# A recurrent layer beside a dense matmul stream: state-free products moved out of the chunk loop, and the loop run in step with the next head pair's products

## The chip, the cores and the metric

The kernel runs on one core of a Trainium2 chip. The metric is device microseconds of one execution, the median of three runs. The core has five engines with a queue each, and each queue runs its instructions in the order in which they were built: TensorE (PE) multiplies matrices into PSUM, VectorE (DVE) and ScalarE (ACT) do elementwise work and read PSUM, GpSimd (POOL) does a little elementwise work, and SyncE (SP) issues the DMAs.

## The reference

One decoder layer over 512 tokens of width 2048, all in float32. What is computed:

- `z = rmsnorm(x) @ w_in`. Half of the columns feed an RG-LRU branch (a short convolution, two gates, a linear scan over time). The others, mixed with the token before, feed an RWKV-7 branch of 16 heads of width 64.
- For each head the RWKV-7 branch keeps a 64x64 state: `state = state * w_t + (state @ -kk_t) b_t^T + v_t k_t^T`, and `y_t = state @ r_t`. A norm of y by head, a bonus term and a gate follow.
- `h = x + concat(out_a, out_b) @ w_o`, a gated feed-forward block of width 6144 with a short convolution, a gated embedding block, and a last norm.

## The kernel before, in words

**Dense stream.** Every large product is made of 128x128x512 matmuls. A float32 weight tile of 128x1024 arrives by DMA and is split into two float32r parts: ACT writes the high part (`whi`, line 118) and DVE the rest (`wlo`, line 119). Each weight block is then multiplied three times (`dense`, lines 148, 150, 152). Phase 1 (`phase1`, about the first 900 us) makes z, the two branches and the part of the output product that is ready by then; phase 2 is the rest of the layer and is almost wholly dense.

**Eight head pairs.** The 16 heads are handled as 8 pairs j, 128 partitions each. `rwkv_z` makes k, r and v of a pair in the dense stream. `prep(j)` makes decays, the normed key and the tiles `AR`, `bt`, `ktl`. `core(j)` runs the recurrence in 8 chunks of 64 tokens, in three stages:

- scores: four batches of matmuls (line 676), masked by DVE into `MQ` and `NQ` (line 678);
- the inverse `TT` of a triangular 64x64 matrix for each chunk: DVE makes 2x2 blocks (lines 699 to 701), then four doublings of two products each on 32x32 tiles (line 708), each followed on DVE by a mask (`Gm`, line 718) or by an addition and a transpose (`Tm`, `Tt`, lines 732, 733), and two last products (lines 739, 749). Beside it DVE makes token-major copies of v, b and k (`turn`: one 128x512 transpose, then four of 32x256, lines 684, 689);
- the chunk loop. The state passes from chunk to chunk through three pieces of PE work, with an engine between each: `px` from the state (lines 761, 764), copied by ACT to `xs`; `pu = TT @ xs` (line 776), copied by ACT to `us`; then the state's update (lines 782, 788), scaled and added by DVE into `st` (line 796). The output `y` takes three more products (lines 769, 772, 785).

At the end of a core come a norm by head (lines 803 to 812, with two short PE pieces at lines 825 and 844) and a store.

**The order on PE** is set while the program is built. `merge` walks a model of time: it takes dense matmuls one by one, counts 216 ns for each, and puts in the next piece of `prep` or `core` when the latency that the piece before declared (table `W`) is over. So PE's queue is a fixed sequence, in which some five to seven dense matmuls stand between two pieces. On the other engines the framework's scheduler sets the order, with the priorities that `merge` gives.

```python
            if core is not None and cr <= t:
                    with self.tc.high_priority(offset=self.OFFS):
                        pe, lat = next(core)
                    t += pe
                    cr = t + max(lat, self.PACE)
```

**The RG-LRU branch** (`lru_x`, `lru_y`) adds DVE work in bursts: reciprocals in four pieces (`recip`, line 569), a scan (line 908), a convolution (line 861). `per` in `W` says how many of its 16 steps stand between the pairs.

Of the kernel before, what the change touches and what calls it, by code (L numbers as in the profile page):

```python
# [16 lines left out]
W = dict(offw=0, offp=-100, offl=0, pace=1000, offs=200, offd=100, start=2088, lora=2383, dec=0, rsk=12200, ready=11377, bonus=26772, t0=3419, tg=1322, tt=1448, lx=1000, lu=914, ls=1363, g1=1489, g2=3586, g3=4312, per=[4, 2, 2, 3, 1, 4, 0])  # L17
# [62 lines left out]
class Builder:  # L80
# [22 lines left out]
    def wfill_(self):  # L103
        nc = self.nc
        while self.wn < len(self.wq) and len(self.wt) < self.LOOK:
            src, shape, *own = self.wq[self.wn]
            self.wn += 1
            if self.wraw:
                raw = self.wraw.pop(0)
            else:  # L110
                raw = self.t(self.wp, "wraw", shape, bufs=self.RAW)
                nc.sync.dma_start(raw, src)
# [85 lines left out]
    def build(self):  # L198
# [4 lines left out]
        with ExitStack() as top:  # L203
            cp = top.enter_context(tc.tile_pool(name="cp", bufs=1))
# [26 lines left out]
    def phase1(self):  # L231
# [18 lines left out]
        wst = [("gt", 2), ("gt", 2), ("bv", 2), ("bv", 2), ("AR", 2), ("AR", 2), ("MQ", 1), ("NQ", 1)]  # L250
        self.xr, self.wraw = [], []

        def wload():
            i = len(self.wraw)
            src, shape = self.wq[i]
            if i < len(wst):
                w = self.t(k1, wst[i][0], shape, bufs=wst[i][1])
            else:
                w = self.t(self.wp, "wraw", shape, bufs=self.RAW)
# [25 lines left out]

        self.zs = cp.tile([128, S + 1], F32, name="zs")
        G.memset(self.zs[:, 0:1], 0.0)
        self.zc = cp.tile([128, S + 3], F32, name="zc")
# [3 lines left out]
        self.prepped = {}  # L292
        with self.tc.manual_schedule(engines={mybir.EngineType.PE}):
            self.merge(self.dense_stream(self.order))

    def start(self):
        A = self.A

        order = [("lora",), ("r", 0)]
# [4 lines left out]
        for j in range(1, NP):  # L304
            order.append(("r", j))
            for _ in range(per[j - 1]):
                order.append(lseq.pop(0))
# [31 lines left out]
    def merge(self, dn):  # L339
# [5 lines left out]
        ptime = 0.0  # L345
        self.ptime = None
        pr = cr = 0.0
        while True:
            if prep is None and pj < NP and pj in self.zdone and pj <= cj + 1:
                prep, pr = self.prep(pj), t + W['start']  # L350
                pj += 1
            if core is None and cj < NP and cj in self.prepped:
                core, cr = self.core(cj, self.prepped[cj]), max(t, ptime)
            if core is not None and cr <= t:
                try:
# [3 lines left out]
                    cr = t + max(lat, self.PACE)  # L359
# [4 lines left out]
            if prep is not None and pr <= t:  # L364
                try:
                    with self.tc.high_priority(offset=W['offp']):
                        pe, lat = next(prep)
                    t += pe
                    if self.ptime is not None:
                        ptime, self.ptime = t + self.ptime, None  # L370
                    pr = t + lat
# [3 lines left out]
            if more:  # L375
                try:
                    with self.tc.high_priority(offset=self.OFFD):
                        next(dn)
# [4 lines left out]
            if core is None and prep is None and cj >= NP:  # L383
                break
            t = min(x for x, g in ((cr, core), (pr, prep)) if g is not None)

    def dense_stream(self, order):
        nc, A = self.nc, self.A
        done = max(i for i, o in enumerate(order) if o[0] == "y")
        for i, o in enumerate(order):  # L390
# [12 lines left out]
            else:  # L403
                if o[1] == 0:
                    self.out_b(range(4, NP - 1))
# [12 lines left out]
    def derive(self):  # L418
# [4 lines left out]
        der = k1.tile([128, 128], F32, name="der")  # L423
# [57 lines left out]
    def lora_z(self):  # L481
# [25 lines left out]
        for tt in range(4):  # L507
            z = self.t(k1, ("vk", "bk", "kk2", "Tm")[tt], (128, LW), bufs=1)
# [44 lines left out]
    def rwkv_z(self, j):  # L553
        k1 = self.k1
        d = {}
        for n, m_, o_ in (("kt", "mu_k", "mk"), ("rt", "mu_r", "mr"), ("vt", "mu_v", "mv")):
            ps = self.mm()
# [14 lines left out]
    def prep(self, j):  # L572
# [35 lines left out]
        psg = wk()  # L608
        for i, (wt, x0) in enumerate(((lh[:, 2, :], self.g0h), (lh[:, 2, :], self.g0l), (ll[:, 2, :], self.g0h))):
            TE.matmul(psg, wt, x0, start=i == 0, stop=False)  # L610
        TE.matmul(psg, lh[0:96, 3, :], self.g1, start=False, stop=True)
        gt = T("gt", 2)
        SC.activation(gt, psg, AF.Copy)
# [9 lines left out]
        pc = T("pc", 2, (128, NC))  # L623
# [4 lines left out]
        yield 2000, W['rsk']  # L628
# [648 lines left out]
```

## Time and profile before

| | |
|---|---|
| median of three runs | 2790.03 us (2787.96 to 2790.09) |
| the profiled execution's own time | 2788.58 us |
| its span | 2786.5 us |
| PE busy over the span | 2739.8 us (98%) |
| DVE busy | 1349.5 us (48%) |
| ACT busy | 895.6 us (32%) |

The profile shows one execution. A row of a timeline gives the start and the length of an instruction, or of several like it (x4). A PE row's length covers the passage through the array, so that neighbouring matmuls overlap: what a matmul costs the queue is the distance from its start to the next one's. The trace shows each small float32 matmul of the program as two instructions. "PE idle" is time in which no matmul was in the array.

### The profile page before, as it was taken

The numbers are of one execution on the slowest core, as the hardware profiler recorded it, in microseconds if no ns is written. First come the engines' busy times: TensorE is split into PE (matmuls) and PEld (weight loads), VectorE is DVE, ScalarE is ACT, GpSimd is POOL, SyncE is SP. The second block draws the span as 40 slices with busy tenths as digits, with TensorE's granted clock in tenths as the row PEclk, the third lists the DMA queues.
The fourth block names the chain that finished last, engine by engine and source line by source line (L and its number), as shares of the span: only waits on it lengthen the run. The fifth ranks groups of instructions, "written<-read, shape, count | busy, mean of one in ns | idle before, by whom it ended". The sixth has DMA issues, their size and how long they took to land.

```text
span 2786.5 us, 42621 instructions
## 1 busy us (share of the span) xinstructions
PE 2739.8 (98%) x18392; PEld 2195.7 (79%) x18392; DVE 1349.5 (48%) x1793; ACT 895.6 (32%) x1352; POOL 291.4 (10%) x232
## 2 busy tenths in 40 slices
PE   8999999999999999999999999999999999999996
PEld 7777777777777888888888888888888888877886
DVE  7786686677673533333333433334333333344235
ACT  6343343434422422212221222222222212234334
POOL 4010010101121310000000000000000000012013
PEclk9999999999999999999999999999999999999998
DMA  5222222222332322222222222222222223223222
GB/s 169 80 69 77 73 73 66 66 69 69 100 119 92 110 97 93 98 99 98 98 92 99 93 96 98 99 98 94 95 96 94 98 98 99 97 90 112 98 89 101
DMA packets 81885, 261.31 MB, mean 94 GB/s; under 512 B 9504, under 2 KB 12192, under 8 KB 81696
## 3 DMA queue, kind: packets, MB, share of 16 engines
q1 hardware_dynamic: 81696, 258.58, 28.1%
q8 instruction: 144, 2.36, 0.4%
q14 instruction: 45, 0.37, 0.0%
HBM read 250.42 MB, written 8.13 MB: 93 GB/s over the span
## 4 chain that ended last, share of the span: by engine, by line
PE 92%; DVE 4%; issue 1%; POOL 1%; ACT 1%; DMA 1%; SPq 0%; DVEq 0%; POOLq 0%; ACTq 0%
PE mm L150 26%; PE mm L152 26%; PE mm L148 26%; PE mm L1120 2%; PE mm L1122 2%; PE mm L1121 2%; PE wk L708 1%; DVE wlo L119 1%; PE wk L676 1%; PE ch L776 1%; PE ch L761 1%; PE y L785 1%; DVE e L1153 0%; PE wk L825 0%; POOL lt L478 0%
## 5 line engine op out<-in xcount | busy, mean ns | idle before, releaser
L118 ACT ACTIVATE whi<-wraw 128x1024 fp32r<-128x1024 f32 (+2 forms) x449 | 468.6, 1044 | 1443.0 <-PE mm L150 1280.4
L119 DVE TENSOR_TENSOR wlo<-wraw,whi 128x1024 fp32r<-128x1024 f32 (+2 forms) x449 | 555.5, 1237 | 495.7 <-ACT whi L118 490.5
L148 PE MATMUL mm<-uh,whi 128*128 128x512 f32 x1536 | 597.7, 389 | 0.0
L152 PE MATMUL mm<-uh,wlo 128*128 128x512 f32 x1536 | 597.6, 389 | 0.0
L150 PE MATMUL mm<-ul,whi 128*128 128x512 f32 x1536 | 597.5, 389 | 0.0
L150 PE MATMUL mm<-xl,whi 128*128 128x512 f32 x1216 | 486.3, 400 | 0.0
L148 PE MATMUL mm<-xh,whi 128*128 128x512 f32 x1216 | 485.3, 399 | 0.9 <-DVE hT L408 0.9
L152 PE MATMUL mm<-xh,wlo 128*128 128x512 f32 x1216 | 486.0, 400 | 0.0
L152 PEld LDWEIGHTS mm<-uh,wlo 128*128 128x128 f32 x1536 | 288.4, 188 | 60.0
L150 PEld LDWEIGHTS mm<-ul,whi 128*128 128x128 f32 x1536 | 288.4, 188 | 59.8
L148 PEld LDWEIGHTS mm<-uh,whi 128*128 128x128 f32 x1536 | 288.4, 188 | 59.7
L148 PEld LDWEIGHTS mm<-xh,whi 128*128 128x128 f32 x1216 | 228.6, 188 | 49.7 <-issue 2.2
L150 PEld LDWEIGHTS mm<-xl,whi 128*128 128x128 f32 x1216 | 228.5, 188 | 49.1 <-issue 2.1
L152 PEld LDWEIGHTS mm<-xh,wlo 128*128 128x128 f32 x1216 | 228.5, 188 | 48.6 <-issue 2.3
L1068 DVE TENSOR_TENSOR hT<-hT,mm 128x512 f32<-128x512 f32 x96 | 66.0, 688 | 321.4 <-PE mm L152 321.4
L1048 POOL TENSOR_TENSOR tmp<-tmp,rsa 128x512 f32<-128x512 f32 x48 | 62.0, 1292 | 1406.6 <-ACT tmp L1047 1406.6
L150 PE MATMUL mm<-hl,whi 128*128 128x512 f32 x384 | 153.4, 400 | 0.0
L152 PE MATMUL mm<-hh,wlo 128*128 128x512 f32 x384 | 152.2, 396 | 0.0
L148 PE MATMUL mm<-hh,whi 128*128 128x512 f32 x384 | 152.1, 396 | 0.0
L1052 DVE TENSOR_TENSOR tmp<-tmp,mm 128x512 f32<-128x512 f32 x48 | 33.0, 688 | 160.2 <-PE mm L152 158.1
L1042 DVE TENSOR_TENSOR gz<-mm,rsa 128x512 f32<-128x512 f32 x48 | 33.2, 692 | 153.9 <-PE mm L152 153.9
L1120 PE MATMUL mm<-whi,uh 128*128 128x512 f32 (+1 forms) x304 | 107.0, 352 | 0.0
(430 smaller groups left out, 2914.0 us busy)
## 6 DMA issues: line engine op xcount, KB each, us to landing
wraw<-wgu SPq DMA_DIRECT2D x192, 512.0 KB, 3.2
wraw<-wd SPq DMA_DIRECT2D x96, 512.0 KB, 3.2
wraw<-wz SPq DMA_DIRECT2D x80, 512.0 KB, 3.6
wraw<-wpg SPq DMA_DIRECT2D x31, 512.0 KB, 3.2
wraw<-wo SPq DMA_DIRECT2D x24, 512.0 KB, 3.3
wraw<-wo SPq DMA_DIRECT2D x16, 256.0 KB, 2.9
tmp<-xT SPq DMA_DIRECT2D x16, 256.0 KB, 2.7
out<-e SPq DMA_DIRECT2D x16, 256.0 KB, 2.5
```

The costliest lines, as they stand in the source:

```text
L118: nc.scalar.activation(hi, raw, AF.Copy)
L119: nc.vector.tensor_tensor(lo, raw, hi.bitcast(F32), ALU.subtract)
L148: nc.tensor.matmul(ps, hi[:, k, :], xh, start=first and i == 0, stop=False)
L150: nc.tensor.matmul(ps, hi[:, k, :], xl, start=False, stop=False)
L152: nc.tensor.matmul(ps, lo[:, k, :], xh, start=False, stop=last and i == n - 1)
L1042: V.tensor_tensor(gz[:, 2:S + 2], pg, rs, ALU.mult)
L1048: G.tensor_tensor(c, c, rs, ALU.mult)
L1052: V.tensor_tensor(c, c, pu, ALU.mult)
L1068: V.tensor_tensor(hT[m], hT[m], pd, ALU.add)
L1120: TE.matmul(pg[tt], u3[k + i][0][:, ts_], wh[:, i, :], start=k + i == 0, stop=False)
L1121: TE.matmul(pg[tt], u3[k + i][0][:, ts_], wl[:, i, :], start=False, stop=False)
L1122: TE.matmul(pg[tt], u3[k + i][1][:, ts_], wh[:, i, :], start=False, stop=k + i == KT - 1)
```

## The change

- `core` is split in two generators. `batch(j)` holds all that needs no state: scores, inverse, token-major copies, and three batches of 64x64 products that are new (`each`): `X1 = NQ^T v`, `WT` (from the token-major copy `ak` of the key row of `AR`, and `TT`), and `TT` applied to `X1`. `chain(j)` is the chunk loop, which now has two pieces in a chunk: `pu = WT^T st`, to which DVE adds the `X1` of the chunk and so gives `us`; then the state's update. ACT's copies `xs` and `us` are gone.
- `duo(j)` runs `chain(j - 1)` and `batch(j)` in step: one piece of each is put into PE's queue together. The last `chain` runs alone.
- `turn` is as before, and is called four times in place of three (`ak` is new).
- `AR` of the next pair is written only when the running `duo` is through; the dense stream holds its place until a pair is prepared (`need`). The norm becomes a generator of its own (`norm`). The numbers of `W` are others, and the RG-LRU steps are spread 2, 3, 2, 2, 2, 2, 3.
- Buffers: `MQ`, `NQ`, `vk`, `bk`, `kk2` twice; some tiles move to another pool.

```diff
-W = dict(offw=0, offp=-100, offl=0, pace=1000, offs=200, offd=100, start=2088, lora=2383, dec=0, rsk=12200, ready=11377, bonus=26772, t0=3419, tg=1322, tt=1448, lx=1000, lu=914, ls=1363, g1=1489, g2=3586, g3=4312, per=[4, 2, 2, 3, 1, 4, 0])
+W = dict(offw=10000, offp=[0, 0, 2000, 2000, 74, 0, 0], offl=0, offt=0, pace=433, dpace=1779, late=4035, offs=20000, offd=0, start=2863, lora=2837, dec=0, rsk=25495, ready=14000, bonus=26772, t0=3322, tg=2489, tt=1500, lx=3454, lu=739, ls=643, g1=684, g2=3586, g3=5015, per=[2, 3, 2, 2, 2, 2, 3, 0])
...
-                    cr = t + max(lat, self.PACE)
+                    cr = t + max(lat, W['dpace'] if 0 < cj < NP else self.PACE)
...
+    def duo(self, j):
+        two = []
+        if j:
+            two.append(self.chain(j - 1, self.prepped[j - 1], self.batched.pop(j - 1)))
+        if j < NP:
+            two.append(self.batch(j, self.prepped[j]))
+        while two:
+            pe, lat = 0, 0
+            for g in list(two):
+                try:
+                    p_, l_ = next(g)
+                    pe, lat = pe + p_, max(lat, l_)
...
+        def each(lhs, rhs, dst):
+            ps = wk()
+            for c in range(NC):
+                for hs in H2:
+                    TE.matmul(ps[hs, c * C:(c + 1) * C], lhs(hs, c), rhs(hs, c), start=True, stop=True)
+            SC.activation(dst, c3(ps), AF.Copy)
...
+        for half in range(2):
+            scores(bt, MQ, half)
...
+                    ak = turn("ak", fl(AR[:, 0]), 1)
...
+        X1 = NQ[:, :, 0:64]
+        each(lambda hs, c: NQ[hs, c, 0:64], lambda hs, c: vk[hs, c, :], X1)
...
+        WT = MQ[:, :, 0:64]
+        each(lambda hs, c: ak[hs, c, :], lambda hs, c: TT[hs, c, :], WT)
+        each(lambda hs, c: TT[hs, c, :], lambda hs, c: NQ[hs, c, 0:64], X1)
...
             if c:
-                for hs in H2:
-                    TE.matmul(px[hs, 0:64], AR[hs, c, 0, :], st[hs], start=False, stop=True)
-            xs = T("xs", 2, (128, 64))
-            SC.activation(xs, px[:, 0:64], AF.Copy)
...
+                pu = ch()
+                for hs in H2:
+                    TE.matmul(pu[hs, 0:64], MQ[hs, c, 0:64], st[hs], start=True, stop=True)
+                us = T("us", 2, (128, 64))
+                V.tensor_tensor(us, pu[:, 0:64], NQ[:, c, 0:64], ALU.add)
...
-            pu = ch()
-            for hs in H2:
-                TE.matmul(pu[hs, 0:64], TT[hs, c, :], xs[hs], start=True, stop=True)
-            us = T("us", 2, (128, 64))
-            SC.activation(us, pu[:, 0:64], AF.Copy)
```

In the new kernel the scores are at line 723 (mask 725), `each` at 732, the 2x2 blocks at 755 to 757, the doublings at 764 (mask 774, addition 792, transpose 793), the last products at 801 and 814, and `turn` at 738 and 743; in the chain `pu` is at 843, `us` at 845, the state's update at 849 and 858, the output's products at 851, 854 and 869, and `st` at 862 and 866. The norm's PE pieces are at 901 and 920.

**PE's queue, one chunk of the loop.** Before (head pair 1; `ch`, `wk` and `y` are PSUM tiles, lines 148 to 152 are dense matmuls):

```order
L761 MATMUL ch_2908<-vk_2360,NQ_2222 64x64 x2
L764 MATMUL ch_2908<-st_2891,AR_1673 64x64 x2
L769 MATMUL y_2769<-NQ_2222,vk_2360 64x64 x2
L772 MATMUL y_2769<-AR_1673,st_2891 64x64 x2
L148 MATMUL mm_2759<-xh_76_380,whi_2648 128x512
...
L776 MATMUL ch_2924<-xs_2913,TT 64x64 x2
L782 MATMUL ch_2929<-vk_2360,kk_396_2555 64x64 x2
L152 MATMUL mm_2759<-xh_81_403,wlo_2649 128x512
...
L785 MATMUL y_2769<-MQ_2221,us_2927 64x64 x2
L788 MATMUL ch_2929<-us_2927,bk_2453 64x64 x2
```

And in the changed kernel (chunk of pair 1 with the products of pair 2):

```order
L843 MATMUL ch_3602<-st_3552,MQ_2070 64x64 x2
L849 MATMUL ch_3607<-vk_2190,kk_370_2576 64x64 x2
L851 MATMUL y_3270<-NQ_2071,vk_2190 64x64 x2
L854 MATMUL y_3270<-AR_1954,st_3552 64x64 x2
L764 MATMUL wk_3614<-Tm_3304,MQ_3282 32x16 x32
L148 MATMUL mm_3401<-xh_85_423,whi_3260 128x512
...
L858 MATMUL ch_3607<-us_3605,bk_2453 64x64 x2
L869 MATMUL y_3270<-MQ_2070,us_3605 64x64 x2
L764 MATMUL wk_3675<-Gm_3647,Tt_3305 32x16 x32
```

Three runs of small matmuls in a chunk, five dense ones between them, have become two, 9 to 12 apart, and each of the two ends with a batch of 32x32 products that stood alone before.

**DVE's queue, from the masks of the scores to `Tm`.** Before (head pair 2):

```order
L678 TENSOR_TENSOR MQ_3303<-wk_3326,con_157 128x512
L812 TENSOR_TENSOR y_510_3227<-y_510_3227,gt_1413 128x512
L699 TENSOR_TENSOR Tt_3372<-MQ_3303,con_157 32x256 x4
L678 TENSOR_TENSOR NQ_3304<-wk_3341,con_157 128x512
L700 TENSOR_TENSOR Tt_3372<-Tt_3372,con_157 128x256
L701 STREAM_TRANSPOSE Tm_3371<-Tt_3372 128x256
```

And in the changed kernel (`lrc` and `lxl` are tiles of the RG-LRU branch, `kk_533` is the copy `kk2`):

```order
L983 TENSOR_SCALAR lrc_4053<-lrc_4053 128x512
L738 STREAM_TRANSPOSE kk_533_3778<-ktl_3174 128x512
L725 TENSOR_TENSOR MQ_3282<-wk_3284,con_157 128x512
L984 SCALAR_TENSOR_TENSOR lxl_444_3104<-lrc_4053,lxl_446_3113 128x512
L725 TENSOR_TENSOR MQ_3282<-wk_3294,con_157 128x512
L738 STREAM_TRANSPOSE ak_3527<-AR_3176 128x512
L755 TENSOR_TENSOR Tt_3305<-MQ_3282,con_157 32x256 x4
L743 STREAM_TRANSPOSE ak_3527<-AR_3176 32x8x32
L756 TENSOR_TENSOR Tt_3305<-Tt_3305,con_157 128x256
L743 STREAM_TRANSPOSE kk_533_3778<-ktl_3174 32x8x32
L845 TENSOR_TENSOR us_3331<-ch_3328,NQ_2071 128x64
L757 STREAM_TRANSPOSE Tm_3304<-Tt_3305 128x256
```

The transposes of the token-major copies and the chain's `us` now stand among the instructions that lead to `Tm`, on which the first doubling product waits.

## Rows read from the trace of the kernel before

**Rows 1.** The page: span, and busy time by engine.
```profile
span 2786.5 us, 42621 instructions
PE 2739.8 (98%) x18392; PEld 2195.7 (79%) x18392; DVE 1349.5 (48%) x1793; ACT 895.6 (32%) x1352; POOL 291.4 (10%) x232
```
**Rows 2.** Busy time by engine in stretches (us, instructions), granted clock, DMA.
```profile
core 0: us, PE busy (x) PEld busy (x) DVE busy (x) ACT busy (x) POOL busy (x), PEclk, DMA share, GB/s
100.00:900.00 800.00, 788.11 (x9543) 580.84 (x9542) 547.11 (x891) 298.31 (x537) 101.15 (x78) 1.00 0.25 79
1000.00:1500.00 500.00, 500.00 (x2198) 412.51 (x2197) 187.16 (x203) 129.49 (x143) 21.96 (x17) 1.00 0.29 97
760.00:775.00 15.00, 15.00 (x125) 10.73 (x123) 14.97 (x21) 4.30 (x10) 3.31 (x2) 1.00 0.49 158
```
**Rows 3.** What PE waited for between 100 and 900 us.
```profile
PE wk L708 <- DVE Gm L718: 7.0, 6, 2.9
PE wk L708 <- DVE Tm L732: 1.5, 4, 0.5
```
**Rows 4.** Timeline of PE: two pieces of a chunk among dense matmuls.
```profile
451.64 0.40 PE L150 MATMUL mm<-xl,whi 128*128 128x512 f32 x1
451.97 0.33 PE L785 MATMUL y<-MQ,us 64*64 64x64 f32 x4
452.13 0.28 PE L788 MATMUL ch<-us,bk 64*64 64x64 f32 x4
452.35 0.50 PE L152 MATMUL mm<-xh,wlo 128*128 128x512 f32 x1
452.69 0.40 PE L148 MATMUL mm<-xh,whi 128*128 128x512 f32 x1
...
453.84 0.39 PE L152 MATMUL mm<-xh,wlo 128*128 128x512 f32 x1
454.16 0.33 PE L761 MATMUL ch<-vk,NQ 64*64 64x64 f32 x4
454.32 0.28 PE L764 MATMUL ch<-st,AR 64*64 64x64 f32 x4
454.44 0.28 PE L769 MATMUL y<-NQ,vk 64*64 64x64 f32 x4
454.56 0.28 PE L772 MATMUL y<-AR,st 64*64 64x64 f32 x4
454.77 0.50 PE L148 MATMUL mm<-xh,whi 128*128 128x512 f32 x1
455.11 0.39 PE L150 MATMUL mm<-xl,whi 128*128 128x512 f32 x1
```
**Rows 5.** Costliest groups of DVE between 100 and 900 us, shapes apart.
```profile
L119 DVE TENSOR_TENSOR wlo<-wraw,whi 128x1024 fp32r<-128x1024 f32 x86 | 116.5, 1355 | 25.6 <-ACT whi L118 25.2
L569 DVE RECIPROCAL th<-th 128x128 f32<-128x128 f32 x28 | 25.1, 926 | 0.2
L689 DVE STREAM_TRANSPOSE bk<-bt 32x256 f32<-32x256 f32 x32 | 13.7, 427 | 0.4
L796 DVE SCALAR_TENSOR_TENSOR st<-ch,pc,so 128x64 f32<-128x64 f32 x48 | 13.4, 278 | 36.3 <-PE ch L788 35.3 <-ACT gt L613 0.3
L684 DVE STREAM_TRANSPOSE bk<-bt 128x512 f32<-128x512 f32 x8 | 5.6, 704 | 0.0
```
**Rows 6.** The same for ACT: the copies of the chunk loop.
```profile
L778 ACT ACTIVATE us<-ch 128x64 f32<-128x64 f32 x64 | 14.0, 219 | 55.5 <-PE ch L776 55.3
```
**Rows 7.** Timeline of DVE: three instructions without a wait between.
```profile
368.86 0.66 DVE L640 TENSOR_TENSOR kt<-kt,ta 128x512 f32<-128x512 f32 x1
369.44 0.68 DVE L909 TENSOR_TENSOR lt<-lt,zc 128x512 f32<-128x512 f32 x1
370.05 2.30 DVE L119 TENSOR_TENSOR wlo<-wraw,whi 128x1024 fp32r<-128x1024 f32 x1
```
**Rows 8.** What DVE waited for between 90 and 720 us.
```profile
DVE Sq L837 <- POOL hmy L835: 7.7, 6, 1.8
```

More of the change, by code (lines that the diff above doesn't have):

```diff
@@ L303, in start @@
         per = W['per']
-        for j in range(1, NP):
+        for j in range(NP):
             order.append(("r", j))
-            for _ in range(per[j - 1]):
+            for _ in range(per[j]):
                 order.append(lseq.pop(0))
@@ L374, in merge @@
                 continue
-            if more:
+            if more and (need is None or need in self.prepped or need in self.outs):
                 try:
                     with self.tc.high_priority(offset=self.OFFD):
-                        next(dn)
+                        need = next(dn)
                     t += MMT
@@ L382, in merge @@
                 continue
-            if core is None and prep is None and cj >= NP:
+            if core is None and prep is None and cj > NP and not self.tails:
                 break
-            t = min(x for x, g in ((cr, core), (pr, prep)) if g is not None)
+            t = min([x for x, g in ((cr, core), (pr, prep)) if g is not None and not (g is prep and late)] + [x[1] for x in self.tails])
     def dense_stream(self, order):
@@ L642, in prep @@
         V.tensor_tensor(ktl, kt, ip, ALU.mult)
+        ready = self.now + W['ready']
+        yield 600, None
+        AR = T("AR", 2, (128, 2, NC, C))
+        V.scalar_tensor_tensor(AR[:, 0], c3(kk), -1.0, pp[:, :, 0:C], ALU.mult, ALU.mult)
+        V.tensor_tensor(AR[:, 1], c3(rt), pp[:, :, 1:C + 1], ALU.mult)
+        psg = wk()
+        for i, (wt, x0) in enumerate(((lh[:, 2, :], self.g0h), (lh[:, 2, :], self.g0l), (ll[:, 2, :], self.g0h))):
+            TE.matmul(psg, wt, x0, start=i == 0, stop=False)
+        TE.matmul(psg, lh[0:96, 3, :], self.g1, start=False, stop=True)
+        gt = T("gt", 2)
+        SC.activation(gt, psg, AF.Copy)
         G.tensor_tensor(rt, rt, kt, ALU.mult)
@@ L648, in prep @@
         self.prepped[j] = (AR, bt, ktl, vt, pc, bv, gt)
-        self.ptime = W['ready']
-        yield 600, W['bonus']
+        self.ptime = max(ready, self.now + W['late'])
+        yield 1100, W['bonus']
         psb = wk()
@@ L733, in core @@
             V.transpose(fl(Tt), fl(Tm))
+            if b == 2:
+                scores(ktl, NQ, 1)
             yield 1100, W['tt']
@@ L797, in core, with norm @@
                 st = sn
-            yield 300, W['ls']
-        y = T("y1")
-        sq = T("Sq")
+            for hs in H2:
+                TE.matmul(yo[hs], us[hs], MQ[hs, c, 64:128], start=False, stop=True)
+            yield 500, W['ls']
+        y, sq = T("y1"), T("Sq")
         SC.activation(sq, py, AF.Square)
-        yield 0, W['g2']
+        SC.activation(y, py, AF.Copy)
+        self.tails.append([self.norm(j, y, sq, bv, gt), self.now + W['g2']])
+    def norm(self, j, y, sq, bv, gt):
+        nc, k1 = self.nc, self.k1
+        V, SC = nc.vector, nc.scalar
         mb = self.head_rs(self.head_ss(sq), 1.0 / 64, LNX_EPS, "y", sq)
@@ L812, in core @@
         V.tensor_tensor(y, y, gt, ALU.mult)
+        self.outs.add("out%d" % j)
         if j < NP - 1:
```

162 lines of the change are left out of this document (92 added, 70 removed).

## The prediction

> **What bounds the kernel now.** I began with the page. PE is busy for 2739.8 of 2786.5 us [rows 1]; no other engine is over half. So the time is the length of PE's queue, plus the places where the queue stands still. The second view is busy time by stretch [rows 2]. From 1000 to 1500 us, in phase 2, PE is never idle, and 2198 instructions take 500 us: one dense matmul each 0.227 us. The change touches nothing there. From 100 to 900 us, where all head pairs run, PE is busy for 788.1 of 800 us: 11.9 us of standing still are all that better hiding could win, and most of them are waits for the masks and additions of the doublings, 7.0 and 1.5 us [rows 3]. The clock is granted in full (1.00) in both stretches. So a gain has to come from fewer or cheaper entries in PE's queue, and a loss from new waits in it.
>
> The third view is PE's timeline around the pieces of a chunk [rows 4], because a busy share hides what a small piece costs. The dense matmul at 451.64 is followed by a run of two groups (785, 788), and the second dense matmul after the run starts at 452.69: 1.05 us, where two dense spacings would be 0.455. The run costs 0.595. From 453.84 to 455.11 the run has four groups, and costs 1.27 - 0.455 = 0.815. Inside a run a group follows the one before after 0.12 us (454.32, 454.44, 454.56). So two groups are worth 0.24 and the other 0.35 is paid once per run: the small matmul starts late (0.33 after the dense one, not 0.227), and the first dense matmul after it takes 0.34. I call the entry and the exit a **crossing** of array shapes, and price one at 0.175 us.
>
> **The change, part by part.**
>
> *PE, crossings.* In the order of before, PE's queue goes into a run of 64- or 32-wide matmuls and out again 304 times, 608 crossings. In the changed order there are 132 runs, 264 crossings, because a chunk has two pieces in place of three and a piece of the chain and one of the batch share a run. But inside the shared runs the queue changes between 64-wide and 32-wide matmuls 94 times, which before never happened. No row shows such a change. Bounds from the nearest rows: nothing, if only leaving the dense shape costs; 0.35, if each change is as dear as a whole excursion. I take 0.175, since in the rows each change of shape costs about that at either end. Saved: (608 - 264 - 94) x 0.175 = 44 us; with free inner changes 60, with dear ones 27.
>
> [...]
>
> *PE, matmuls.* The chunk loop loses two products in most chunks; the three new batches bring 16 each. By count of the order, 64x64 matmuls go from 960 to 1088. A group is two of them, so 128 x 0.06 = 8 us more. The scores and the doublings stay. Net on PE: 44 - 8 = **36 us less**, between 19 and 52.
>
> *ACT.* 128 copies of 0.22 us [rows 6] are gone, from the path of the state; 24 copies out of PSUM come in `each`. ACT is far from full (298 of 800 us [rows 2]), so I cost this at nothing; should `X1` come late, the chain's `us` would be late next.
>
> *DVE, work.* Eight calls of `turn` for `ak`: 8 x (0.70 + 4 x 0.43) = 19 us [rows 5]. 56 additions for `us`, priced as the `st` of the same shape: 56 x 0.28 = 16 us. DVE gets 35 us more, on 547 of 800: about 582 of some 765, 76%. On average that is covered. It isn't where the work is bunched: from 760 to 775 DVE is already busy for 14.97 of 15 us, with no harm to PE [rows 2].
>
> *DVE, the bunch ahead of `Tm`.* This is the term that decides. PE's order is fixed when the program is built, so if DVE is behind when PE reaches the first doubling product of a pair, PE stands still, and everything dense behind it too. I went through DVE's new queue for each pair, from the last instruction at which DVE still has to wait for PE, up to the transpose that gives `Tm`, and set the instructions' durations against PE's work between the same two points. For pair 2 the stretch runs from the scaling of an RG-LRU product (line 933) to `Tm`: 68 instructions, among them 12 reciprocals at 0.93 and 7 `wlo` at 1.355 [rows 5], together 51.6 us by the mean of each line. PE has 170 dense matmuls between (38.6 us) and some 3.9 us of small ones, by the prices above: 42.5 us. The means overstate: in an unbroken row an instruction starts about 0.07 us before the end of the one ahead (0.66 long, 0.58 apart; 0.68 long, 0.61 apart [rows 7]). So the stretch needs 51.6 - 68 x 0.07 = 46.9 us, and PE would wait 4.4 us. The same count gives, for pairs 0 to 7: 0.3, 3.2, 4.4, 0.7, 2.8, 1.9, 2.4 and none, together **16 us**. With the means unshortened, and the worst starting point for each pair, it gives 47 us. Shortened is nearer, since the rows show the overlap; but such a stretch also holds a wait for POOL's power of the norm, 7.7 us in six such waits before [rows 8], 1.3 each. Seven of them make 9. I take 16 + 9 = **25 us**, between 16 and 56.
>
> *DVE, the chain.* `us` now stands in DVE's queue, where a `wlo` of 1.36 us (once 2.30 [rows 7]) can be ahead of it; what queues behind a late `us` is the chain's update and the 32-wide batch in the same run. Nine dense matmuls (2.0 us) and the rest of the run lie between, where before there were five; I cost it at nothing, and leave the 11.9 us of idle PE time as it is. The last chain, alone with 3 or 4 dense matmuls between its pieces, has less cover; up to 5 us could come from there.
>
> *DMA, SP, POOL.* The same transfers, the same count on POOL; nothing on either is waited for in the rows.
>
> **The sum.** -36 + 25 = -11 us on the profiled execution's 2788.58. The median of the runs is 1.45 us above it: 2790.03 - 11 = **2779 us**. In this case alone the time lies between 2768 and 2790.
>
> **Rivals.**
>
> 1. *DVE keeps up.* The scheduler that ordered DVE's queue put the transposes where it saw room, and in the loop itself DVE's new queue is light, so a backlog may drain before PE needs it. Against it: the stretches ahead of `Tm` are longer than PE's by the rows, even shortened. Then at most 5 us are lost, and 36 to 52 saved: 2743 to 2759, about 2753.
>
> 2. *Slower: the backlog of DVE outweighs PE's saving.* Place: the first doubling product of each pair, waiting for `Tm`. Price: 47 us by the unshortened means plus 9 for POOL, 56; -36 + 56 = +20, 2810 us. It decides from the point where the waits of the eight pairs come to over 36 us. For it: DVE is the engine that got 35 us, part of it ahead of the masks and among the steps to `Tm`; and shortening the queue of PE leaves DVE less time to hide in. Against it: the unshortened prices deny the overlap that rows 7 show, and in the stretch from 760 us DVE ran at 14.97 of 15 us without PE waiting.
>
> 3. *The inner changes of shape are dear.* At 0.35 each PE saves 27 - 8 = 19 us, and DVE takes 25 back, some of it less since PE is slower: +6 at most, about 2793, no change that can be measured.
>
> That the change doesn't do what it says is ruled out by the order: the copies `xs` and `us` of ACT are gone, and chain and batch share their runs.
>
> **How the numbers follow.** A measurement of this kernel can tell 0.2% from no change, 5.6 us: faster is below 2784.4, slower above 2795.6. The forecast has a chance of 0.42, of which 0.28 lies below 2784.4 and 0.14 within. Rival 1 has 0.28, all faster. Rival 2 has 0.22, 0.21 of it slower and 0.01 within. Rival 3 has 0.08, 0.06 within and 0.02 slower. So faster 0.56, same 0.21, slower 0.23. The range reaches from the middle of rival 1 to the end of rival 2, 2746 to 2810: outside are the best of rival 1 (inner changes free, DVE in time) and what lies above its price in rival 2, together under 0.2.
>
> **What would show it.** Right, if the timeline of PE after shows two runs in a chunk, a dense matmul 0.34 long after each, about 0.15 to 0.2 us between the last 64-wide and the first 32-wide start beyond their usual spacing, and if the waits of PE list the doubling product (line 764) waiting for `Tm` (line 757) with some 20 to 30 us in about seven waits. Rival 1 is right if PE's idle time from 100 to 870 us stays near 12 us. Rival 2 if it exceeds 48 us. The count of crossings is wrong if PE's busy time falls by much less than 36 us. The whole is wrong if PE waits in new places: for `us` in most chunks, for `X1`, for `wlo`, or where phase 2 begins.

## The result and the profile after

The changed kernel takes **2799.94 us** (median of 6 runs, 2797.20 to 2802.25); the kernel before, run beside it, 2787.94 us (6 runs). The ratio is 1.0041, 95% interval [1.0028, 1.0054]: slower by 0.4%, some 12 us. The profiled execution's own time is 2802.25 us, against 2788.58 us before.

The page of after, span and busy time by engine, for [rows 1]:

```profile
span 2800.5 us, 43093 instructions
PE 2717.9 (97%) x18648; PEld 2225.1 (79%) x18648; DVE 1375.8 (49%) x1889; ACT 886.5 (32%) x1249; POOL 292.6 (10%) x232
```

PE's busy time fell by 21.9 us while the span rose by 14.0. Busy time by stretch, for [rows 2] (us, busy us and instructions by engine, granted clock, DMA); the last two are the 16 us around one wait:

```profile
100.00:900.00 800.00, 753.82 (x9732) 599.68 (x9732) 565.18 (x975) 284.26 (x427) 101.72 (x78) 0.96 0.25 77
1000.00:1500.00 500.00, 500.00 (x2205) 412.94 (x2205) 187.74 (x203) 131.04 (x145) 24.08 (x18) 1.00 0.29 96
...
322.00:331.00 9.00, 1.06 (x18) 0.54 (x16) 8.84 (x17) 0.35 (x1) 1.67 (x1) 0.83 0.23 69
331.00:338.00 7.00, 6.89 (x90) 5.66 (x90) 5.68 (x12) 1.78 (x2) 0.00 (x0) 0.50 0.01 2
```

Phase 2 is as it was. From 100 to 900 us PE now stands still for 46.2 us (11.9 before), and the granted clock, 1.00 before, is 0.96. The two short stretches show why: PE does almost nothing for 9 us while DVE is busy for 8.84 of them, and in the next 7 us PE works, but at a granted clock of 0.50. What PE waited for over the whole span, for [rows 3] (total us, times, longest):

```profile
PE wk L764 <- DVE Tm L757: 31.6, 7, 7.6
PE wk L901 <- ACT tmp L621: 4.1, 1, 4.1
PE y L869 <- DVE us L845: 4.0, 3, 1.9
...
PE wk L764 <- DVE us L845: 2.5, 1, 2.5
```

31.6 + 2.5 = 34.1 us of waiting are at the first doubling product of a pair, once in each of the eight pairs: 2.0, 6.2, 7.6, 2.5, 4.5, 3.2, 4.8 and 3.3 us. PE's timeline at the longest of them, to be read beside [rows 4]:

```profile
322.79 0.33 PE L843 MATMUL ch<-st,MQ 64*64 64x64 f32 x4 [0.41 <-DVE st L862]
322.96 0.28 PE L849 MATMUL ch<-vk,kk 64*64 64x64 f32 x4
323.07 0.28 PE L851 MATMUL y<-NQ,vk 64*64 64x64 f32 x4
323.19 0.28 PE L854 MATMUL y<-AR,st 64*64 64x64 f32 x4
331.11 1.05 PE L764 MATMUL wk<-Tm,MQ 32*32 32x16 f32 x64 [7.64 <-DVE Tm L757]
332.09 1.97 PE L723 MATMUL wk<-AR,ktl 64*64 64x128 f32 x16
333.99 0.79 PE L150 MATMUL mm<-xl,whi 128*128 128x512 f32 x1
334.59 0.63 PE L152 MATMUL mm<-xh,wlo 128*128 128x512 f32 x1
335.01 0.63 PE L148 MATMUL mm<-xh,whi 128*128 128x512 f32 x1
...
351.08 0.28 PE L854 MATMUL y<-AR,st 64*64 64x64 f32 x4
351.29 0.73 PE L764 MATMUL wk<-Tm,MQ 32*32 32x16 f32 x64
351.95 0.50 PE L148 MATMUL mm<-xh,whi 128*128 128x512 f32 x1
352.29 0.39 PE L150 MATMUL mm<-xl,whi 128*128 128x512 f32 x1
```

After the wait dense matmuls start 0.42 apart, and the doubling batch takes 0.98 to the next start; at 351.29 the same batch takes 0.66, and dense matmuls elsewhere are 0.23 apart. Ahead of another wait (6.17 us, ending at 213.24) PE's scores for `MQ` are through by about 201.4:

```profile
199.52 1.92 PE L723 MATMUL wk<-AR,bt 64*64 64x128 f32 x32
```

DVE from there on, to be read beside [rows 7]:

```profile
201.98 0.70 DVE L738 STREAM_TRANSPOSE ak<-AR 128x512 f32<-128x512 f32 x1
202.71 0.43 DVE L743 STREAM_TRANSPOSE bk<-bt 32x256 f32<-32x256 f32 x1
...
207.05 0.40 DVE L743 STREAM_TRANSPOSE kk<-ktl 32x256 f32<-32x256 f32 x1
207.48 1.29 DVE L725 TENSOR_TENSOR MQ<-wk,con 128x512 f32<-128x512 f32 x2
208.68 1.22 DVE L119 TENSOR_TENSOR wlo<-wraw,whi 128x1024 fp32r<-128x1024 f32 x1
209.82 1.70 DVE L755 TENSOR_TENSOR Tt<-MQ,con 32x256 f32<-32x256 f32 x4
211.55 0.69 DVE L933 TENSOR_TENSOR row<-mm,rs 128x512 f32<-128x512 f32 x1
212.16 0.21 DVE L845 TENSOR_TENSOR us<-ch,NQ 128x64 f32<-128x64 f32 x1
212.29 0.41 DVE L756 TENSOR_TENSOR Tt<-Tt,con 128x256 f32<-128x256 f32 x1
212.74 0.45 DVE L757 STREAM_TRANSPOSE Tm<-Tt 128x256 f32<-128x256 f32 x1
```

The copies' transposes stand ahead of the masks `MQ`, with no idle time between: they are needed only several steps later, and PE waits for what is behind them. It is not so in every pair. From the end of the scores for `MQ` to `Tm` DVE's timeline holds about 17 us of copies' transposes over the eight pairs, and about 23 us of other instructions that do not lead to `Tm` (the RG-LRU branch, `wlo`, `prep` and the chain). Pair 4, with a wait of 4.46 us, has 0.7 us of copies there and 5.3 us of the others.

**A balance.** From the first matmul of line 177 in phase 2 onwards the kernels are alike (1802.5 us are left to the end of the span before, 1801.1 after):

```profile
999.36 0.83 PE L177 MATMUL wk<-con,acc 128*128 128x1 f32 x7
```

Before, this point lies at 984.0 us. The waits in the brackets of PE's timeline up to it, without the 1.45 us ahead of PE's first matmul, sum to 20.0 us before and 54.6 after. The rest is the time in which PE did not wait: 964.0 and 944.8 us. So +15.4 = 34.6 of waits - 19.2 of rest.

The rest mixes PE's work with the clock at which it was done. Up to line 177 the changed kernel has 61.4 us at a granted clock of 0.50, and PE has a matmul in the array for 49.1 of them; before, 3.4 us. A dense matmul takes 0.43 there in place of 0.23, so half of these 49.1 us, 24.6, is an estimate of what the half clock added (rather too much, since the doubling batch is slowed less: 0.98 against 0.66 above). The column "half" gives this estimate for each run, "work" the rest less "half". "For Tm" is the sum of the waits of the first doubling product for the transpose that makes `Tm`; "clock" is the granted one from 100 to 900 us. Each ratio is to the kernel before, run beside that run.

| kernel | median us | ratio to before | for Tm | up to L177 | waits | rest | clock | half | work |
|---|---|---|---|---|---|---|---|---|---|
| before | 2787.94 | | 0 | 984.0 | 20.0 | 964.0 | 1.00 | 1.7 | 962.3 |
| after | 2799.94 | 1.0041 [1.0028, 1.0054] | 31.6 | 999.4 | 54.6 | 944.8 | 0.96 | 24.6 | 920.2 |
| 1 cover | 2777.78 | 0.9962 [0.9949, 0.9974] | 6.0 | 976.4 | 41.3 | 935.1 | 0.98 | 13.7 | 921.4 |
| 2 fill | 2800.15 | 1.0039 [1.0025, 1.0052] | 8.0 | 999.6 | 34.4 | 965.2 | 0.98 | 13.8 | 951.4 |
| 3 no ak | 2789.13 | 1.0001 [0.9992, 1.0010] | 29.1 | 985.0 | 48.9 | 936.1 | 0.97 | 16.0 | 920.1 |
| 4 not in step, cover | 2798.10 | 1.0038 [1.0025, 1.0052] | 0 | 991.5 | 38.1 | 953.4 | 0.99 | 9.0 | 944.4 |
| 5 scores back | 2792.84 | 1.0018 [1.0009, 1.0027] | 0 | 991.4 | 54.6 | 936.8 | 0.97 | 11.6 | 925.2 |
| 6 work to ACT | 2813.02 | 1.0089 [1.0076, 1.0103] | 34.3 | 1010.1 | 61.5 | 948.6 | 0.96 | 29.2 | 919.4 |
| 7 before, moved | 2826.95 | 1.0138 [1.0122, 1.0153] | 17.4 | 1022.9 | 47.9 | 975.0 | 0.98 | 18.0 | 957.0 |
| 8 = 5 and 6 | 2778.94 | 0.9968 [0.9956, 0.9981] | 0 | 976.5 | 42.7 | 933.8 | 0.99 | 7.5 | 926.3 |
| 9 held copies | 2774.67 | 0.9946 [0.9929, 0.9962] | 17.5 | 971.5 | 37.1 | 934.4 | 0.98 | 14.0 | 920.4 |
| 10 held, cover | **2755.55** | 0.9877 [0.9862, 0.9892] | 2.3 | 951.2 | 22.5 | 928.7 | 0.99 | 8.2 | 920.5 |
| 11 before, held | 2802.05 | 1.0044 [1.0029, 1.0059] | 0 | 995.3 | 26.1 | 969.2 | 0.99 | 6.1 | 963.1 |
| 12 = 10, not in step | 2807.15 | 1.0066 [1.0049, 1.0082] | 0 | 1002.1 | 47.6 | 954.5 | 0.98 | 11.9 | 942.6 |
| 13 Tm late by 12 | 2812.29 | 1.0082 [1.0067, 1.0097] | 53.0 | 1003.5 | 67.7 | 935.8 | 0.96 | 17.0 | 918.8 |
| 14 Tm late by 24 | 2863.19 | 1.0266 [1.0249, 1.0283] | 100.9 | 1060.2 | 113.1 | 947.1 | 0.92 | 28.3 | 918.8 |

The kernels that give PE the changed kernel's work (after, 1, 3, 6, 9, 10, 13, 14) agree in "work" to 918.8 to 921.4 us, while their rest goes from 928.7 to 948.6. That supports the estimate, which divides the change of the time up to line 177: +15.4 = 34.6 of waits + 22.9 of half clock - 42.1 of PE's work.

### The profile page after: what moved, and what is told of

It is laid out like the page before. It is cut to its first block, busy times and chain, and to the rows that moved or that the text cites. A ratio compares the mean times of both kernels' runs of the same rounds, so it can differ in the third digit from the quotient of the medians.

```text
span 2800.5 us, 43093 instructions
## 1 busy us (share of the span) xinstructions
PE 2717.9 (97%) x18648; PEld 2225.1 (79%) x18648; DVE 1375.8 (49%) x1889; ACT 886.5 (32%) x1249; POOL 292.6 (10%) x232
## 4 chain that ended last, share of the span: by engine, by line
PE 86%; DVE 9%; issue 1%; DMA 1%; POOL 1%; ACT 1%; SPq 0%; DVEq 0%; POOLq 0%; ACTq 0%
PE mm L150 24%; PE mm L148 24%; PE mm L152 24%; PE mm L1199 2%; PE mm L1197 2%; PE mm L1198 2%; PE wk L764 2%; DVE wlo L119 1%; PE wk L723 1%; DVE lrc L595 1%; PE wk L732 1%; DVE Tt L755 0%; DVE th L595 0%; PE wk L901 0%; DVE e L1230 0%
## 5 line engine op out<-in xcount | busy, mean ns | idle before, releaser
L1119 DVE TENSOR_TENSOR row<-mm,rsa 128x512 f32<-128x512 f32 x48 | 33.2, 692 | 153.9 <-PE mm L152 153.9
L1199 PE MATMUL mm<-whi,ul 128*128 128x512 f32 (+1 forms) x304 | 106.4, 350 | 0.0
```

The costliest lines, as they stand in the source:

```text
L1119: V.tensor_tensor(gz[:, 2:S + 2], pg, rs, ALU.mult)
L1199: TE.matmul(pg[tt], u3[k + i][1][:, ts_], wh[:, i, :], start=False, stop=k + i == KT - 1)
```

## The experiments

### More cover, or the waits filled (1, 2)

```diff
-t0=3322
+t0=8000
```

(out of the line of `W`)

> The changed kernel with one number of the table W altered: the latency declared between the scores and the first doubling product (t0) is 8000 in place of 3322, so that 38 dense matmuls stand there in PE's queue for each pair in place of 16 (5 us more of cover). Nothing is added to or taken from any engine's work. Theory (the waits of the first doubling product for Tm come from DVE being behind, and the half clock of TensorE follows from these waits): the waits of line 764 for Tm fall from 31.6 us to under 8, the granted clock from 100 to 900 us goes back from 0.96 to 0.99 or more, and the time falls by 25 (waits) plus some 12 to 17 (clock): 2758 to 2768 us, faster than both kernels. Rival (the waits are the price of running chain and batch in step, and only move to a later product, or the half clock comes from the mixed small matmuls themselves): waits and clock stay as they are in sum, time within 6 us of 2800.

Measured: 2777.78 us, 22 us off the changed kernel and faster than the kernel before. The waits for `Tm` are 6.0 us. The time fell less than expected (2758 to 2768): the clock came back to 0.98 and not to 0.99, and another wait came, at 671.5 us:

```profile
PE mm L148 <- DVE row L951: 9.2, 1, 9.2
PE wk L764 <- DVE Tm L757: 6.0, 3, 2.6
```

A dense matmul there waits for DVE to empty a PSUM tile. So distance in PE's queue alone, with no work taken from DVE, removes four fifths of the waits for `Tm`.

```diff
+FILL = 16
...
+            if b == 2:
+                fps = wk()
+                for i in range(FILL):
+                    TE.matmul(fps, self.xs[0][0][:, 0:128], self.xs[0][0], start=i == 0, stop=i == FILL - 1)
```

> The changed kernel with 16 dense matmuls per pair added just ahead of the first doubling product; they multiply two tiles that are there anyway into a PSUM tile that nobody reads. 8 x 16 x 0.227 = 29 us of PE work are added, and nothing moves on DVE. Theory (waits and clock are two costs, the second following the first): the filling takes the place of the waiting (sum of the eight waits 34, of which 3.6 us each can be filled: some 26 us), so idle time falls to about 20 us in the first 900 us, the clock is granted in full, and the time falls by what the half clock cost, 12 to 17 us, less 3 to 6 us of filling that met no wait: 2785 to 2794 us. If the half clock has another cause than the waits: it stays at 0.96 and the time is 2800 to 2806 us. If there is no wait for DVE to be filled at all: 2829 us.

Measured: 2800.15 us. The waits fell by 20.2 us for 29 us of filling. Of the rest, 965.2 - 29 = 936.2 us are the kernel's own, 8.6 less than in the changed kernel. The time lies where the expectation put another cause of the half clock, but the clock rose to 0.98, which that cause ruled out. It came back in part only, so this run alone did not settle what the half clock comes from.

### Less work for DVE (3, 6)

```diff
-                    ak = turn("ak", fl(AR[:, 0]), 1)
...
-        each(lambda hs, c: ak[hs, c, :], lambda hs, c: TT[hs, c, :], WT)
+        each(lambda hs, c: MQ[hs, c, 0:64], lambda hs, c: TT[hs, c, :], WT)
```

> The changed kernel without the token-major copy ak (five transposes per pair, 2.4 us of DVE each time); the product WT reads the masked scores MQ in its place, so that the output is another. PE's queue has the same work. Theory (DVE's backlog makes the waits for Tm): in the stretches seen in the trace ak's transposes stand ahead of Tm, so each of the seven long waits gets up to 2.4 us shorter: the waits fall from 31.6 to 14 to 18 us, the clock rises to 0.97 to 0.99, the time falls by 15 to 30 us to 2770 to 2785. Rival (the waits don't depend on how much DVE has to do; DVE stands behind ACT, POOL or PE there): waits within 4 us of 31.6, time within 6 us of 2800.

Measured: 2789.13 us, between the ranges of the theory and of the rival, and 29.1 us of waits for `Tm`: 18 us less on DVE (1357.7 against 1375.8 us busy) took 5.7 us from all waits. The theory that the waits measure DVE's load fails. The rest is 8.7 us shorter (936.1 against 944.8), by the estimate all of it less half clock.

```diff
-            V.tensor_scalar(rc, t1, -1.0, 1.0, ALU.mult, ALU.add)
+            SC.activation(rc, t1, AF.Copy, scale=-1.0, bias=1.0)
...
-        V.tensor_scalar(th, th, -1.0, 1.0, ALU.mult, ALU.add)
+        SC.activation(th, th, AF.Copy, scale=-1.0, bias=1.0)
```

(and the same for the two of 2x - 1)

> The changed kernel with 32 instructions taken from DVE and given to ACT: 1 - x and 2x - 1 of the decays and of the RG-LRU branch (lines 636, 640, 975, 983), 17 us of DVE by the rows of after (6.2 + 2.7 + 1.6 + 3.4 + 3.4), and with them two stalls of DVE for POOL, 2.4 us. PE's queue is the same. They stand in the bursts just ahead of the masks of the scores. Theory (the waits come from too little cover between the masks and Tm; DVE's load in all matters little, as when ak was taken out: 19 us less on DVE, 5 us less waiting): idle time falls by 3 to 10 us, time 2785 to 2797. Rival (DVE's load in the bursts ahead of the masks makes the waits): waits for Tm fall below 15 us, half-clock stretches with them, time 2765 to 2782.

Measured: 2813.02 us, 13 us slower than the changed kernel, with 34.3 us of waits for `Tm`. Both expectations were wrong: 18 us less on DVE (1357.9 us busy) made nothing shorter, and PE now waits for ACT and DVE at a product of the RG-LRU gates as well:

```profile
PE wk L764 <- DVE Tm L757: 34.3, 7, 8.5
PE mm L961 <- ACT lxh L131: 4.8, 2, 2.5
PE mm L963 <- DVE lxl L132: 4.1, 2, 3.0
```

### The move of the scores, undone and done alone (5, 7, 8)

```diff
-        for half in range(2):
-            scores(bt, MQ, half)
+        for src, dst in ((bt, MQ), (ktl, NQ)):
+            for half in range(2):
+                scores(src, dst, half)
+                yield 1080, 0
...
-            if b == 2:
-                scores(ktl, NQ, 0)
...
-            if b == 2:
-                scores(ktl, NQ, 1)
```

> The changed kernel with one part of the change undone: the four batches of scores are again four pieces of their own, all ahead of the first doubling product, as in the kernel before (in step with the pieces of the chain). Between the second batch for MQ and the first doubling product PE's queue then has 31 dense matmuls and two batches of scores, as the kernel before had, in place of 16 dense matmuls. DVE's work is the same to the instruction. Theory (moving the batches for NQ behind the first doubling product took 5 us of cover away from the path from the masks to Tm, and that, not DVE's 35 us more, made the waits): waits of line 764 for Tm under 8 us, time within 6 us of the 2777.8 that the run with 38 dense matmuls gave, 2771 to 2784 us. Rival (DVE is behind by its load; cover only shifts where it shows): waits of 15 us or more for Tm or for other products of DVE in the batch, 2785 to 2800 us.

Measured: no wait for `Tm` is left, as the theory says, but the time is 2792.84, in the rival's range: other waits came, one of them 16.5 us. This run gives more cover than the expectation says: between the second batch for `MQ` and the first doubling product PE's timeline has 25 dense matmuls in the first pair and 40 or 41 in the others, not 31, since the pieces of a step stand further apart. So it doesn't give back the lost cover alone.

```profile
PE wk L723 <- DVE ktl L659: 16.5, 1, 16.5
PE ch L840 <- DVE st L859: 7.8, 3, 4.1
PE mm L148 <- DVE row L948: 7.6, 1, 7.6
```

DVE's timeline ahead of the 16.5 us shows `ktl`, which the moved scores need, behind a burst of the RG-LRU branch and transposes of copies:

```profile
676.55 3.39 DVE L595 RECIPROCAL lrc<-lrc 128x128 f32<-128x128 f32 x4
679.97 0.44 DVE L743 STREAM_TRANSPOSE bk<-bt 32x256 f32<-32x256 f32 x1
680.33 0.40 DVE L743 STREAM_TRANSPOSE ak<-AR 32x256 f32<-32x256 f32 x1
...
684.55 1.68 DVE L659 TENSOR_TENSOR ktl<-kt,th 128x512 f32<-128x512 f32 x1
```

> The kernel before with one part of the change alone: both batches of scores for MQ in one piece, the first doubling product after the latency t0 (16 dense matmuls), and the batches for NQ behind the first and the second doubling product, as in the changed kernel. Nothing else of the change is there: no ak, no us on DVE, no step. On PE it saves 3 runs per pair (24 x 0.35 = 8 us) and adds some 24 inner changes (2 us). Theory (this move takes the cover away): waits for Tm at the first doubling product appear, 12 to 30 us in all against 1.5, some half-clock stretches after them, time 2789 - 6 + 12 to 30 + 3 to 10: 2798 to 2823 us. Rival (the waits need DVE's additional work or the step): waits for Tm stay below 6 us, time 2780 to 2790.

The edit of the kernel before is the same move in the other direction. Measured: 2826.95 us, 38 us slower than before, more than expected. The first product waits for `Tm` in all eight pairs:

```profile
PE wk L708 <- DVE Tm L701: 17.4, 8, 5.1
PE wk L675 <- DVE bt L637: 10.0, 3, 5.2
```

There is no `ak`, no `us` on DVE and no step in this kernel. So the move of `NQ`'s batches behind the first product is by itself enough to make waits there, if not all 31.6 us of them. The rest rose as well (975.0 against 964.0). By the estimate that is half clock, 18.0 us in place of 1.7, less 5.3 us of work, where 6 were expected.

> Both edits of this call on the changed kernel: scores all ahead of the first doubling product, and the 32 instructions on ACT. Theory: what waits are left in the first run's twin (41 us idle where 20 are from the kernel before) are DVE late in other places, so DVE's 17 us less give some of it back: 2 to 8 us faster than the scores alone, 2765 to 2778 us. Rival (what is left has nothing to do with DVE's load, or ACT becomes late): equal within 3 us or slower.

Measured: 2778.94 us, 14 us better than the scores alone, where the ACT edit alone cost 13. One edit with opposite signs in two surroundings suggests that the order into which the scheduler then puts DVE's queue matters more than DVE's total; what in that order made the difference was not tried.

### The copies held back (9, 10, 11)

```diff
             d_ = T(n, bufs, (128, NC, C))
+            SC.activation(d_[:, 0, 0:1], Gm[:, 0, 0:1], AF.Copy)
             V.transpose(fl(d_), src)
```

> The changed kernel with the 20 transposes of a pair held back: ACT first writes one column of each copy's tile from the first mask Gm, so that no transpose of the pair can be put ahead of the masks, Tt and Tm on DVE (32 small ACT instructions more; DVE's and PE's work the same). DVE's order then goes from the masks for MQ to Tm with nothing of the copies between. Theory (16 dense matmuls are too little cover for what DVE has been given between the scores and Tm, and the copies' transposes are the larger part of that): waits for Tm fall from 31.6 to 8 to 18 us, slow stretches with them, 2768 to 2787 us. Rival (DVE is late by what came before the scores, the copies fill what would be idle anyway): waits for Tm stay over 24 us, 2792 to 2802 us.

Measured: 2774.67 us, 17.5 us of waits for `Tm`, both as the theory says. DVE has the same 1889 instructions, with no copy between the scores for `MQ` and `Tm` in any pair, and 25 us went. What is left is mostly in three pairs, 2, 4 and 6, with 4.31, 5.12 and 5.01 us. There instructions of the RG-LRU branch and `wlo` are what stands between, and in pairs 4 and 6 holding the copies took nothing off the waits (4.46 and 4.83 in the changed kernel):

```profile
496.15 1.05 PE L765 MATMUL wk<-Tm,MQ 32*32 32x16 f32 x64 [5.12 <-DVE Tm L758]
```

> The held copies and t0 = 8000 together (38 dense matmuls between the scores and the first doubling product). Theory: no wait for Tm over 1 us is left; the doublings get the transposes beside them, and with 8 dense matmuls for each step there is room for five more; 2762 to 2776 us, faster than cover alone (2777.8) by 2 to 14 us. Rival (the copies only move the wait to the doublings' masks or to X1): equal to cover alone or slower, with waits of line 764 for Gm or of line 732 over 8 us.

Measured: **2755.55 us**, 1.2% faster than the kernel before and 44 us faster than the change as it was made, below the range expected, though one wait for `Tm` of 1.58 us is left. Its page, and its stretches:

```profile
span 2752.3 us, 43105 instructions
PE 2702.7 (98%) x18648; PEld 2215.0 (80%) x18648; DVE 1376.1 (50%) x1889; ACT 890.2 (32%) x1279; POOL 297.0 (11%) x232
...
100.00:900.00 800.00, 783.81 (x9945) 626.14 (x9944) 601.51 (x1024) 311.25 (x492) 116.27 (x86) 0.99 0.27 84
```

DVE is as busy as in the changed kernel (1376.1 and 1375.8 us), and PE stands still for 16.2 of 800 us.

> The kernel before with its copies held back in the same way (ACT writes a column of vk, bk and kk2 from the first mask Gm before DVE transposes): is the gain of holding the copies a property of the changed kernel, or would the kernel before have had it too? Theory: in the kernel before only 1.5 us of waits for Tm are there to win, and 31 dense matmuls and two batches of scores cover the masks; time within 5 us of before, 2784 to 2795 us. Rival (holding the copies helps in itself): 10 us or more faster, under 2780.

Measured: 2802.05 us, 13 us slower: neither expectation. The kernel before gets two long waits at the norm (`tmp`, line 838; 9.5 us) instead. Holding the copies is no gain in itself; it is one for this order.

### What the step saves (4, 12)

```diff
-        while two:
-            pe, lat = 0, 0
-            for g in list(two):
...
+        for g in two:
+            yield from g
...
-dpace=1779, lu=739, ls=643
+dpace=1000, lu=914, ls=1363
```

(the last two out of the line of `W`)

> The products of a pair in one batch are kept, the step is undone: duo runs all pieces of the chain of the pair before, and then all pieces of the batch, each piece in a place of its own in PE's queue (the spacing of pieces 1000 in place of 1779, lu and ls 914 and 1363 as in the kernel before), with the cover t0 = 8000 of the first run of this call. PE's queue then goes into a run of small matmuls 81 times more than with the step, and has no change between 64-wide and 32-wide in a run. Theory (a run costs 0.35 for its two crossings, an inner change 0.1): 81 x 0.35 - 94 x 0.1 = 19 us slower than the first run of this call, 2777 to 2787 us, with full clock and short waits. Rival (in step is what costs: DVE serves two pieces at a time): faster than the first run of this call, or within 4 us of it.

Measured: 2798.10 us, 20.3 slower than run 1; the rest grew by 953.4 - 935.1 = 18.3 us, where 19 were expected. That agreement is in part luck. The trace keeps 24 of the 94 inner changes, which the expectation took all away; by its prices and the trace's count of 83 more runs that is 83 x 0.35 - 70 x 0.1 = 22 us, and with less half clock in this run PE's work grew by 944.4 - 921.4 = 23.0.

> The run with held copies and cover (2755.5 us), with the step undone as in the run not in step: first all pieces of the chain, then all of the batch. With the waits gone from both, the difference is what the step saves on PE. By the order: 434 changes into or out of small matmuls against 268, 24 inner changes against 94. Theory (0.175 for each outer change, 0.1 for each inner one): 166 x 0.175 - 70 x 0.1 = 22 us slower, 2772 to 2783 us, with waits and clock as in the run with the step. Rival (the step saves nothing once DVE is in time): 2750 to 2763 us.

Measured: 2807.15 us. The rest grew by 954.5 - 928.7 = 25.8 us; of these 3.7 are half clock, and the work is 22.1 (22 expected). The other 25.1 are waits. With the pieces 1000 in place of 1779 apart, `X1` comes 27 to 30 us behind the first doubling product, waits taken off, where it was 33 to 37 in seven of the eight pairs, and the held copy `vk` is late for it (17.2 us in two waits). So the step saves 22 to 23 us of PE's queue. That its longer batch also gives DVE the time for the copies fits this, but spacing and step were changed together.

### Waits made on purpose (13, 14)

```diff
+        for _ in range(12):
+            V.transpose(fl(Tm), fl(Tt))
         V.transpose(fl(Tm), fl(Tt))
```

> The run with held copies and cover (2755.5 us, 22.5 us idle before phase 2, 2.3 us of excess over the usual spacing of PE), and 12 superfluous transposes of Tt into Tm ahead of the last one, for every pair: 12 x 0.36 = 4.4 us of DVE each. By that run's trace Tm was ready 5.4, 4.0, 0, 2.9, 0, 6.0, 0.2 and 4.5 us ahead of the first doubling product, so that waits of 0, 0.4, 4.4, 1.5, 4.4, 0, 4.2 and 0 us come: 15 us. PE's queue is the same. Theory (TensorE's clock falls to half after a wait of some us): about four slow stretches, 2 us each, on top: 2755.5 + 15 + 8 = 2778 us, excess 8 to 12 us. Rival (the half clock has another cause): 2770 us, excess 2 to 4 us.

> The same with 24 superfluous transposes, 8.7 us of DVE for each pair: waits of 3.3, 4.7, 8.7, 5.8, 8.7, 2.7, 8.5 and 4.2 us, 47 us in all. Theory: eight slow stretches of some 2 us, 2755.5 + 47 + 17 = 2819 us, excess 15 to 22 us. Rival (another cause): 2802 us, excess 2 to 4 us.

Measured: 2812.29 and 2863.19 us, both far above the theory's times. The waits were larger than I had worked out, 45.2 and 90.6 us more than in run 10, because the transposes start 0.48 apart and other instructions of DVE came between them. What they were for is in the rest: 7.1 us more with 12 and 18.4 more with 24, where the theory had 8 and 17 and the rival nothing. PE's queue is the same in the three runs, instruction by instruction, and so is its work (920.5, 918.8, 918.8). PE's timeline after one of the waits of run 14:

```profile
353.64 1.05 PE L767 MATMUL wk<-Tm,MQ 32*32 32x16 f32 x64 [14.56 <-DVE Tm L760]
...
357.54 0.63 PE L150 MATMUL mm<-xl,whi 128*128 128x512 f32 x1
357.97 0.63 PE L152 MATMUL mm<-xh,wlo 128*128 128x512 f32 x1
...
359.43 0.39 PE L148 MATMUL mm<-xh,whi 128*128 128x512 f32 x1
359.66 0.39 PE L150 MATMUL mm<-xl,whi 128*128 128x512 f32 x1
```

0.43 apart, then 0.23. The granted clock is 0.50 from 353.60 to 358.50 and 1.00 from 360 to 364. So in this kernel these waits of PE cost their own length and, after it, work at half the clock.

## Why the prediction was wrong

*PE's work, -36 us: right in kind, 6 us too small.* By the estimate PE's work fell by 42.1 us. The runs, the crossings and the inner changes are as counted (the traces have 304 and 132 runs, and 94 inner changes). The price of an inner change was too high: from the last 64-wide group to the 32-wide batch there are 0.21 us (351.08 to 351.29), against 0.12 between 64-wide groups, so it costs about 0.1, not 0.175. With 0.1 the prediction's sum is 60 - 9 - 8 = 43. Rival 3, which wanted 0.35, fails. PE's busy time fell by only 21.9 us, which the prediction had as a sign of a wrong count; but busy time gets longer at half clock (a dense row is 0.63 long at 335.01, 0.39 at 352.29), by some 23 us here by the same estimate.

*The bunch ahead of `Tm`, +25 us: the place right, the size too small.* The waits are where the text put them, but they are 34.1 us at that product, and all waits rose by 34.6. The count by pair (0.3, 3.2, 4.4, 0.7, 2.8, 1.9, 2.4, none) picked out the pairs that wait longest, and is 1.3 to 3.3 us too small in each; which price in it is too low stays open. The reason given, DVE's new work and a backlog, is only part of it. That work was 31 us by the rows of after (19.1 of `ak`, 12.0 of `us`), not 35; runs 3 and 6 took about half as much off DVE, and the waits for `Tm` stayed at 29 and 34 us. Three things made them. The change moved `NQ`'s batches behind the first product, so that between the last batch for `MQ` and that product 16 dense matmuls are left where there were 31 and two batches of scores; I had listed the scores as staying. The scheduler puts the copies' transposes, which are ready early, ahead of masks that PE is about to wait for. And in some pairs the RG-LRU branch stands there in the same way. More cover alone leaves 6.0 us of waits, holding the copies alone 17.5, both 2.3; the move alone, in the kernel before, makes 17.4. The RG-LRU part is read from the timelines; no run moved that branch.

*The clock: no term at all.* This is the step that turned the sign. I read a clock of 1.00 in both stretches of the kernel before and carried it over, though I forecast seven new waits. The clock from 100 to 900 us is 0.96, and by the estimate half clock cost 22.9 us more than before. Without it the time up to line 177 would have changed by -42.1 + 34.6 = -7.5 us; with it, it is +15.4. Runs 13 and 14 show that waits bring the half clock, with PE's queue unchanged: by the estimate it cost 17.0 and 28.3 us there, and 8.2 in run 10. In the trace of after the clock is 0.50 from 331 to 338 us, behind the wait of 7.64.

*The rivals and the range.* Rival 2 had the place and the sign. With waits at 34.6 it would not have decided by its own bound of 36, and PE's idle time from 100 to 870 us, 45.1, stays under the 48 that were to show it; it did decide because a wait costs more than its length. That the time lies inside the whole range is owed to this rival's end of it, not to the sum. The range itself is not worked out cleanly: the bounds of the two terms give 2754 to 2827 for the forecast's own case, where the text has 2768 to 2790. Rival 1 (DVE in time, 2753 us) is what run 10 made of the kernel: 2755.55. The us additions of the chain, costed at nothing, waited 4.0 us in three places.

The numbers of `W` other than `t0` and, in runs 4 and 12, the spacing, and the new spread of the RG-LRU steps, changed together with the rest; what each of them did was not tried.

## What to carry to other kernels

When a step of a fixed queue is moved, count what is left between each producer on that queue and the consumer that comes back to it through another engine: the move took cover away, and that mattered more than the work that the other engine gained. An instruction that is ready early and needed late can stand ahead of one that is needed now; tie it to a later tile. Price a wait of TensorE above its length: here 34.6 us of waits cost about 57 by the estimate, 34.6 + 22.9. The surcharge is no fixed share of the waits' length: by the estimate it is 22.9 us with these 34.6, and 20.1 us with the 90.6 that run 14 has more than run 10.

## What the runs showed of the hardware

Up to run 12, between 100 us and line 177, the granted clock falls to 0.50 in 74 stretches; 72 of them begin during a wait of PE of 1 us or more, or within 6 us after one. The other way round, such a stretch began with 15 of 64 waits of 1 to 2 us, with 31 of 40 of 2 to 4 us, and with 31 of 32 longer ones. In the changed kernel a wait of 1.92 us that ended at 470.09 was followed by one, and a wait of 1.89 at 386.37 was not. What decides between the two was not tried.
